# A first phase worked tile by tile: keys and queries directly behind their modulation, in a diffusion layer on one Trainium2 core

## The chip, the cores and the metric

The kernel runs on one core of one Trainium2 chip. The metric is the device time in microseconds of one execution. TensorE (PE) multiplies matrices and loads its weights beside that (PEld); VectorE (DVE), ScalarE (ACT) and GpSimd (POOL) work on tiles; the queue of SyncE (SP) issues nearly all transfers (DMA) from the chip's memory, in program order.

## The reference, cut to what matters

One layer with two token mixers over 256 latent tokens `x` and 256 context tokens `ctx`, D = 2048. Both are normalised and modulated by a shift and a scale that come from a conditioning vector through a large matrix, and then multiplied by the columns of `w_in`. The part that the change touches:

```python
mod = (jax.nn.silu(c) @ w_mod[l] + b_mod[l])[:, None, :]
sa, ca, ga, sm, cm, gm = jnp.split(mod, 6, axis=-1)
mod_c = jax.nn.silu(c_ctx) @ w_mod[l] + b_mod[l]
h_c = modulate(x_ctx, norm_attn_w[l], sa_c, ca_c)     # rmsnorm(x, w) * (1 + scale) + shift
k_c = rmsnorm(split_qk(p_c_kv[..., :QK_WIDTH]), k_norm_w[l])
h = modulate(x, norm_attn_w[l], sa, ca)
p = h @ w_in[l]
q = axial_rope(rmsnorm(split_qk(p[..., Q_OFF:K_OFF]), q_norm_w[l]), row, col)
k = axial_rope(rmsnorm(split_qk(p[..., K_OFF:V_OFF]), k_norm_w[l]), row, col)
```

Values, attention, a pooling mixer, gates, an output product and a squared-ReLU MLP follow; the change does not alter what they compute.

## The kernel before

Every product is computed in three matmuls: each operand is split into a high part (a cast on ScalarE) and a low part (a subtraction on VectorE), and `mm3` adds high x high, high x low and low x high.

Phase one walks over 16 *tiles* f of 128 rows of D. For each tile `mod_tile` multiplies four chunks of `w_m` (512 KB each, 32 short matmuls, "mod") into shift and scale for both kinds of tokens; ScalarE copies them out (`rows`), `mod_columns` turns them into columns (`modT` on TensorE, `col` on ScalarE and VectorE), and `hidden(f, 0)` writes the modulated, transposed tile of x (`hL`, high part on ScalarE, low part on VectorE), `hidden(f, 1)` that of the context (`hC`). Products with the first 512 columns of keys and queries accumulate in six banks over the 16 tiles: `kx` (keys of x), `kc` (keys of the context) and `q` (queries of x). One tile k of one of them, two token halves of 128 with three matmuls each, is six matmuls of 512 columns; the prediction calls this a unit. A chunk of `w_k` or `w_q` holds the weights of two tiles, the pair j = k // 2.

The order of work is set in these places:
- `plan` writes the order of all transfers; `load_next` issues the next one, `wchunk` asks for a chunk and has up to `FIRST_AHEAD` = 3 further ones issued in program order ahead. SP issues in that order, and each transfer waits until its buffer is free.
- Buffers: even tiles' w_m and all chunks of w_k and w_q share one ring of five raw buffers. Odd tiles' w_m have buffers of their own (`mod_raw`: one of two chunks, two of one). `first` holds two split chunks of w_k; w_q, one chunk of w_k and later weights go through three `whi`/`wlo`.
- `side` runs through the products in the order of a list, and `PACE` says how many half units each tile issues, half of them ahead of `modT` and half behind it. The pair j is loaded behind the odd tile 2j + 1 (j = 2 behind tile 6), so its products come two tiles or more behind the modulation.
- `square_sums` squares tokens on ScalarE, adds pairs on VectorE and sums over partitions by matmuls with `mean`; for the context this stands behind `mod` of tile 4.
- A scheduler lays out each engine's instructions from this program order, so the rows of other stages can move as well; TensorE's own order is held in phase one (`ordered_pe`).

Behind phase one, `qk_evac` normalises keys and queries on ScalarE, VectorE and GpSimd (`qraw`, `qsq`, `qss`) and TensorE turns them (`qkT`) in the midst of the v products, a number of chunks later that `later` counts. `macc` are parts of other modulation vectors, computed on VectorE beside all of this.

Of the kernel before, what the change touches and what calls it, by code (L numbers as in the profile page):

```python
# [13 lines left out]
AF = mybir.ActivationFunctionType  # L14
# [5 lines left out]
KT = D // P  # L20
T = 256
# [27 lines left out]
def layer(ctx: ExitStack, tc, a, out):  # L49
# [3 lines left out]
    pe, gp = nc.tensor, nc.gpsimd  # L53
# [20 lines left out]
    def work(name, shape=None, dt=F32):  # L74
        return pool.tile(shape or [P, 512], dt, tag="w2", name=name, bufs=9)
# [42 lines left out]
    def chain(*gens):  # L118
        for g in gens:
            yield from g  # L120
# [5 lines left out]
    def plan(name, *idx, rate=0.0):  # L126
        stream.append(((name,) + idx, rate))
# [3 lines left out]
    for f in range(KT):  # L131
        for i in range(4):
            plan("w_m", f, i)
            if f in (2, 3) and i % 2 == 1:
                plan("cT", 2 * f - 4 + i // 2)
            if (f, i) == (9, 0):
                plan("prq")
        j = 2 if f == 6 else -1 if f == 5 or f % 2 == 0 else f // 2
        if j >= 0:
            plan("w_k", 0, j)  # L140
            plan("w_q", 0, j)
    for n, g, rate in (("w_v", 0, 1.5), ("w_q", 1, 1.0), ("w_k", 1, 1.5), ("w_v", 1, 1.5)):
        for ch in range(8):
            plan(n, g, ch, rate=rate)
# [50 lines left out]
    def load_next():  # L195
        key, rate = stream[len(loaded)]
        src = a[key[0]]
        for i in key[1:]:
            src = src[i]
        if key[0] == "prq":  # L200
            nc.sync.dma_start(prq, src)
            loaded.append((key, None, None))
            return
        if key[0] in ("cT", "x"):
            dst = cT[:, 4 * key[1]:4 * key[1] + 4, :] if key[0] == "cT" else x1_tile()[:, key[1], key[2] * 512:key[2] * 512 + 512]
            nc.sync.dma_start(dst, src)
            loaded.append((key, None, None))
            return
        n = src.shape[-1]
        if key[0] == "w_m":  # L210
            raw = mod_raw(*key[1:])
            sp.dma_start(raw, src)
            loaded.append((key, raw, raw))
            return
        raw = raw_chunk(src, n)
        if key[:2] == ("w_k", 0):
            if not first:
                first.append(s16("first", [P, 4, 1024], F32R))
            i = 2 * (key[2] % 2)
            hi, lo = first[0][:, i, :], first[0][:, i + 1, :]  # L220
        else:
            hi = pool.tile([P, n], F32R, tag="whi", name="whi", bufs=3)
            lo = pool.tile([P, n], F32R, tag="wlo", name="wlo", bufs=3)
        act.copy(hi, raw)  # L224
        vec.tensor_sub(lo, raw, hi.bitcast(F32))  # L225
# [30 lines left out]
    def rsq(v, n, div, tag=None):  # L256

        mk = (lambda nm: small(nm, n)) if n <= 16 else (lambda nm: work(nm, [P, n]))
        y = mk(tag or "rq_y")
        pin(act.activation(y, v, AF.Ln, scale=div * 2.0 ** -64, bias=epsb))  # L260
        act.activation(y, y, AF.Exp, scale=-0.5, bias=ebias)
        t = mk("rq_t")
        vec.scalar_tensor_tensor(t, y, -0.5 * div, y, ALU.mult, ALU.mult)
        vec.scalar_tensor_tensor(t, v, EPS / div, t, ALU.add, ALU.mult)
        vec.scalar_tensor_tensor(y, t, 1.5, y, ALU.add, ALU.mult)
        return y
# [102 lines left out]
    def mod_columns(f, rows):  # L369

        pt = bank("modT")
        for a in range(2):
            pe.matmul(pt[:, 2 * a:2 * a + 2], rows[:, a * P:a * P + P], quads, start=a == 0, stop=a == 1,
                      skip_group_check=True)
        col = small("col", 4)
        act.copy(col, pt[:, 0:4])
        c3 = col.rearrange("p (a c) -> p a c", a=2)
        vec.tensor_add(c3, c3, bias2[:, :, f:f + 1].broadcast_to([P, 2, 2]))
        vec.tensor_scalar(c3[:, 0, :], c3[:, 0, :], pr("nw")[:, f:f + 1], None, ALU.mult)
        return c3  # L380

    def hidden(f, t, c3):

        src, h = ((xT, hL), (cT, hC))[t]
        u = work("hw", [P, T])
        ht, k8 = h[f // 8], f % 8
        bias = c3[:, 1, t:t + 1]
        vec.scalar_tensor_tensor(u, src[:, f, :], c3[:, 0, t:t + 1], rms[t], ALU.mult, ALU.mult)
        act.activation(ht[:, 0, k8, :], u, AF.Identity, bias=bias)
        vec.scalar_tensor_tensor(ht[:, 1, k8, :], u, bias, ht[:, 0, k8, :].bitcast(F32), ALU.add, ALU.subtract)  # L390

    def tokens(nt):
        return [(hL, 0), (hL, 1), (hC, 0), (hC, 1)][:nt]

    def xmm(banks, toks, k, hi, lo, sl, first, last):
        for ps, (h, t) in zip(banks, toks):
            mm3(ps, tok(h, k, 0, t), tok(h, k, 1, t), hi[:, sl], lo[:, sl], first, last)
# [61 lines left out]
    def square_sums(src, eng, sb, i):  # L459

        sq = [work("sq") for _ in range(2)]
        for h in range(2):
            k = 4 * i + 2 * h
            xs = src[:, k:k + 2, :].rearrange("p a t -> p (a t)")
            act.activation(sq[h], xs, AF.Square)
        eng.tensor_add(sq[0], sq[0], sq[1])
        return lambda: [pin(pe.matmul(sb[:, 0:T], mean, sq[0][:, h * T:h * T + T], start=(i + h == 0), stop=(i + h == 4)))
                        for h in range(2)]

    fb = {}  # L470
    held = {}

    def pair_steps(n, j):

        w = "w_q" if n == "q" else "w_k"
        if w not in fb:
            fb[w] = [bank(f"{w}_{t}") for t in range(4 if n != "q" else 2)]
        hi, lo = held[w, j]
        for kk in range(2):
            k = 2 * j + kk  # L480
            for t in range(2):
                t4 = t + (2 if n == "kc" else 0)
                xmm([fb[w][t4]], [tokens(4)[t4]], k, hi, lo, slice(kk * 512, kk * 512 + 512), k == 0, k == KT - 1)
                yield

    def steps(n):
        for _ in range(n):
            next(side, None)

    order = [("kx", 0), ("q", 0), ("kx", 1), ("q", 1), ("kc", 0), ("kc", 1), ("kx", 2), ("q", 2), ("kc", 2)]  # L490
    for j in range(3, 7):
        order += [("kx", j), ("q", j), ("kc", j)]
    side = chain(*(pair_steps(*o) for o in order))
    PACE = (0, 0, 4, 4, 6, 6, 8, 8) + (6,) * 8

    cols = {}

    context = {4: (0, 1), 5: (2, 3, 4), 6: (5, 6)}
    ordered_pe[0] = True
    sb = bank("ssq")  # L500
    for i in range(4):
        square_sums(xT, vec, sb, i)()
    rms = [rsq(sb[:, 0:T], T, P / D, "rms")]
    for f in range(KT):
        if f % 2 == 0:
            ps = bank("mod")
        rows = mod_tile(f, ps)
        if f == 4:
            sb = bank("ssq")
            for i in range(4):  # L510
                square_sums(cT, vec, sb, i)()
            rms.append(rsq(sb[:, 0:T], T, P / D, "rms"))
        j = 2 if f == 6 else -1 if f == 5 or f % 2 == 0 else f // 2
        if j >= 0:
            for w in ("w_k", "w_q"):
                held[w, j] = wchunk(w, 0, j, ahead=FIRST_AHEAD if j < 7 else 1)
        steps(PACE[f] // 2)
        cols[f] = mod_columns(f, rows)
        steps(PACE[f] - PACE[f] // 2)
        hidden(f, 0, cols[f])  # L520
        for k in context.get(f, (f,) if f > 6 else ()):
            hidden(k, 1, cols[k])
        if f == 10:
            tables()
    lasts = [pair_steps(n, 7) for n in ("kx", "q", "kc")]
    for _ in range(2):
        for g in lasts:
            next(g)
            next(g)
    ordered_pe[0] = False  # L530
    kb, qb = fb["w_k"], fb["w_q"]
    qT = s8("qT", [P, NH, T])
    kT = s16("kT", [P, NH, 2 * T])
    for t in range(4):
        qk_evac(kb[t], t, 0, kT, 2, 2 + t)
    for t in range(2):
        qk_evac(qb[t], t, 0, qT, 0, 6 + t)

# [552 lines left out]
```

## Time and profile before

| | us |
|---|---|
| median of 3 runs | 1506.75 |
| lowest and highest | 1505.76, 1507.11 |
| the profiled execution | 1506.33 |
| its span, first to last instruction | 1504.5 |
| granted TensorE clock, mean | 0.991 |
| TensorE busy | 1457.1 (97%) |
| phase one ends (first v matmul) | 147.97 |

The page gives busy times of one profiled execution; matmuls are pipelined and the end of one is modelled, so prices are taken from start to start. The granted clock is the share of full speed that TensorE's clock was given. A row of the timeline is: start, length, engine, line, operation, out<-in, count, and in brackets the idle time before it with what ended it. L67 is the line of a helper through which all matmuls of phase one go.

### The profile page before, as it was taken

What the parts mean: (1) busy time and instruction counts of PE and PEld (TensorE: products, weight loads), DVE (VectorE), ACT (ScalarE), POOL (GpSimd) and SP (SyncE); (2) the same over time, 40 slices, a digit from 0 to 9 for tenths busy, and PEclk for the clock granted to TensorE, in tenths of its full rate; (3) what the DMA queues carried; (4) which work ended last, traced back from release to release, by engine and by line L of the source; (5) the groups of instructions that cost most, each with busy time, mean ns of one, the idle gap of its engine ahead of it and who ended that gap; (6) DMA issues with size and microseconds to landing.
All of it is one profiled execution on the core that took longest, in us unless ns stands there. A gap on an engine that the chain in (4) does not pass through costs nothing.

```text
span 1504.5 us, 20036 instructions
## 1 busy us (share of the span) xinstructions
PE 1457.1 (97%) x7592; PEld 1205.5 (80%) x7592; DVE 992.0 (66%) x1216; ACT 694.6 (46%) x956; POOL 120.7 (8%) x120
## 2 busy tenths in 40 slices
PE   5899999999899999999989999999999999999998
PEld 3567787678878888888879988888888888888887
DVE  3465968877877776666766765666666555555575
ACT  3334344646654444444534545535445453544532
POOL 0000101100320000000000100100000010000260
PEclk8999999999999999999999999999999999999999
DMA  9798687366578778788756677677776666656564
GB/s 377 296 345 324 195 284 247 98 210 208 169 234 295 255 262 273 249 304 282 213 159 203 226 247 239 210 248 229 246 236 215 192 189 194 188 192 193 186 194 141
DMA packets 97440, 347.85 MB, mean 231 GB/s; under 512 B 11072, under 2 KB 11712, under 8 KB 97344
## 3 DMA queue, kind: packets, MB, share of 16 engines
q1 hardware_dynamic: 96768, 345.50, 69.6%
q8 instruction: 59, 0.97, 0.3%
q0 software_dynamic: 576, 1.08, 0.2%
q14 instruction: 37, 0.30, 0.1%
HBM read 344.44 MB, written 2.10 MB: 230 GB/s over the span
## 4 chain that ended last, share of the span: by engine, by line
PE 87%; DVE 4%; DMA 4%; ACT 2%; issue 1%; POOL 1%; SPq 0%; DVEq 0%; ACTq 0%; POOLq 0%
PE f L940 14%; PE f L419 8%; PE f L418 8%; PE f L421 8%; PE f L943 7%; PE pg L419 3%; PE pg L418 3%; PE pg L421 3%; DMA raw<-in_w_m_dram 2%; PE w_k L67 2%; PE wo L419 2%; PE wo L421 2%; PE wo L418 2%; PE pyy L418 2%; PE pyy L419 2%; PE pyy L421 2%
## 5 line engine op out<-in xcount | busy, mean ns | idle before, releaser
L225 DVE TENSOR_TENSOR wlo<-raw,whi 128x1024 fp32r<-128x1024 f32 x443 | 547.9, 1239 | 360.4 <-ACT whi L224 337.6
L224 ACT CAST whi<-raw 128x1024 fp32r<-128x1024 f32 x443 | 463.9, 1048 | 574.2 <-PE f L419 184.9
L940 PE MATMUL f<-h,whi 128*128 128x512 f32 x896 | 224.2, 392 | 0.0
L418 PE MATMUL f<-whi,act 128*128 128x512 f32 x512 | 199.4, 389 | 0.0
L419 PE MATMUL f<-whi,act 128*128 128x512 f32 x512 | 199.3, 389 | 0.0
L940 PEld LDWEIGHTS f<-h,whi 128*128 128x128 f32 x896 | 161.7, 189 | 29.3
L581 DVE SCALAR_TENSOR_TENSOR macc<-raw,sil,macc 128x1024 f32<-128x1024 f32 x128 | 167.5, 1308 | 2.2 <-DMA macc<-in_b_ga_dram 1.9
L421 PE MATMUL f<-wlo,act 128*128 128x512 f32 x512 | 136.8, 389 | 0.0
L943 PEld LDWEIGHTS f<-h,wlo 128*128 128x128 f32 x896 | 122.3, 190 | 8.7
L943 PE MATMUL f<-h,wlo 128*128 128x256 f32 x896 | 124.9, 282 | 0.0
L421 PEld LDWEIGHTS f<-wlo,act 128*128 128x128 f32 x512 | 96.1, 188 | 19.9
L418 PEld LDWEIGHTS f<-whi,act 128*128 128x128 f32 x512 | 96.2, 188 | 19.9
L419 PEld LDWEIGHTS f<-whi,act 128*128 128x128 f32 x512 | 96.2, 188 | 19.7
L418 PE MATMUL pg<-whi,hL 128*128 128x512 f32 x256 | 100.6, 393 | 0.0
L419 PE MATMUL pg<-whi,hL 128*128 128x512 f32 x256 | 99.7, 390 | 0.0
L951 POOL TENSOR_TENSOR rsq<-relu 128x512 f32<-128x512 f32 x28 | 29.1, 1041 | 537.2 <-ACT relu L950 516.9
L421 PE MATMUL pg<-wlo,hL 128*128 128x512 f32 x256 | 68.6, 390 | 1.9 <-DVE wlo L225 1.9
L421 PEld LDWEIGHTS pg<-wlo,hL 128*128 128x128 f32 x256 | 48.0, 188 | 12.3 <-DVE wlo L225 2.4
L418 PEld LDWEIGHTS pg<-whi,hL 128*128 128x128 f32 x256 | 48.1, 188 | 10.1 <-issue 0.2
L419 PEld LDWEIGHTS pg<-whi,hL 128*128 128x128 f32 x256 | 48.1, 188 | 10.1 <-issue 0.2
L418 PE MATMUL wo<-whi,mix 128*128 128x512 f32 x128 | 49.9, 390 | 0.0
L419 PE MATMUL wo<-whi,mix 128*128 128x512 f32 x128 | 49.8, 389 | 0.0
(251 smaller groups left out, 2111.3 us busy)
## 6 DMA issues: line engine op xcount, KB each, us to landing
raw<-in_w_ff_dram SPq DMA_DIRECT2D x240, 512.0 KB, 4.3
raw<-in_w_m_dram SPq DMA_DIRECT2D x64, 512.0 KB, 8.0
raw<-in_w_ga_dram SPq DMA_DIRECT2D x32, 512.0 KB, 4.6
raw<-in_w_cm_dram SPq DMA_DIRECT2D x32, 512.0 KB, 4.4
raw<-in_w_gb_in_dram SPq DMA_DIRECT2D x32, 512.0 KB, 4.5
raw<-in_w_ga_in_dram SPq DMA_DIRECT2D x32, 512.0 KB, 4.7
raw<-in_w_sm_dram SPq DMA_DIRECT2D x32, 512.0 KB, 4.8
raw<-in_w_o_dram SPq DMA_DIRECT2D x32, 512.0 KB, 4.3
```

The source lines that it names most:

```text
L67: return (lambda *a, **k: pin(emit(*a, **k))) if self.flag[0] else emit
L224: act.copy(hi, raw)
L225: vec.tensor_sub(lo, raw, hi.bitcast(F32))
L418: pe.matmul(banks[t], tok(h, k, 0, tt), wt, start=k == 0, stop=False)
L419: pe.matmul(banks[t], tok(h, k, 1, tt), wt, start=False, stop=False)
L421: pe.matmul(banks[t], tok(h, k, 0, tt), wt, start=False, stop=k == 2 * nk - 1)
L581: pin(vec.scalar_tensor_tensor(acc, raw, sil[:, 0, k:k + 1], acc, ALU.mult, ALU.add))
L940: pe.matmul(ps, hi[:, kk * P:kk * P + P], both(h2, k), start=k == 0, stop=False)
L943: pe.matmul(ps[:, T:2 * T], lo[:, kk * P:kk * P + P], act_slice(h2, k, 0), start=False, stop=k == KT - 1)
L951: gp.tensor_mul(sq, r, r)
```

## The change

The transfers of a pair of w_k and w_q now stand directly behind the w_m of its even tile. Products of tiles 0 to 3 on x follow directly on their own modulation (`modulate`, then `products`). From tile 4 on, products of an earlier tile come behind `mod`, the first of them ahead of `modT`: context of tiles 0 and 1 at tile 4, then tile f - 1 at tile f, the context catching up at tiles 7 and 8. At the end the products of tile 15 are left, six half units instead of twelve. The context's squares are added up on VectorE (`context_squares`, at tiles 2 and 3) and summed by one matmul. The third pair of w_k goes through `whi` instead of `first`, so the buffers of `first` are numbered anew. The keys' turning is counted one chunk later (3 + t for 2 + t).

```diff
     for f in range(KT):
         for i in range(4):
             plan("w_m", f, i)
-            if f in (2, 3) and i % 2 == 1:
-                plan("cT", 2 * f - 4 + i // 2)
-            if (f, i) == (9, 0):
-                plan("prq")
-        j = 2 if f == 6 else -1 if f == 5 or f % 2 == 0 else f // 2
-        if j >= 0:
-            plan("w_k", 0, j)
-            plan("w_q", 0, j)
+        if f % 2 == 0:
+            plan("w_k", 0, f // 2)
+            plan("w_q", 0, f // 2)
+        if f in (2, 3):
+            plan("cT", 2 * f - 4)
+            plan("cT", 2 * f - 3)
+        if f == 9:
+            plan("prq")
...
-        if key[:2] == ("w_k", 0):
+        if key[:2] == ("w_k", 0) and key[2] != 2:
...
-            i = 2 * (key[2] % 2)
+            i = 2 * ((key[2] - (key[2] > 2)) % 2)
...
-    order = [("kx", 0), ("q", 0), ("kx", 1), ("q", 1), ("kc", 0), ("kc", 1), ("kx", 2), ("q", 2), ("kc", 2)]
-    for j in range(3, 7):
-        order += [("kx", j), ("q", j), ("kc", j)]
-    side = chain(*(pair_steps(*o) for o in order))
-    PACE = (0, 0, 4, 4, 6, 6, 8, 8) + (6,) * 8
...
+    def context_squares(i):
+        sq = [work("sq") for _ in range(2)]
+        for h in range(2):
+            act.activation(sq[h], cT[:, 4 * i + 2 * h:4 * i + 2 * h + 2, :].rearrange("p a t -> p (a t)"), AF.Square)
+        vec.tensor_add(sq[0], sq[0], sq[1])
+        if total:
+            vec.tensor_add(total[0], total[0], sq[0])
+        else:
+            total.append(sq[0])
+
+    behind = [[("kx", f), ("q", f)] for f in range(4)]
+    behind += [[("kc", 0), ("kc", 1)], [("kx", 4), ("q", 4), ("kc", 2)], [("kx", 5), ("q", 5), ("kc", 3)],
+               [("kx", 6), ("q", 6), ("kc", 4), ("kc", 5)], [("kx", 7), ("q", 7), ("kc", 6), ("kc", 7)]]
+    behind += [[(n, f - 1) for n in ("kx", "q", "kc")] for f in range(9, KT)]
...
     for f in range(KT):
         if f % 2 == 0:
             ps = bank("mod")
         rows = mod_tile(f, ps)
-        if f == 4:
-            sb = bank("ssq")
-            for i in range(4):
-                square_sums(cT, vec, sb, i)()
-            rms.append(rsq(sb[:, 0:T], T, P / D, "rms"))
-        j = 2 if f == 6 else -1 if f == 5 or f % 2 == 0 else f // 2
-        if j >= 0:
-            for w in ("w_k", "w_q"):
-                held[w, j] = wchunk(w, 0, j, ahead=FIRST_AHEAD if j < 7 else 1)
-        steps(PACE[f] // 2)
-        cols[f] = mod_columns(f, rows)
-        steps(PACE[f] - PACE[f] // 2)
-        hidden(f, 0, cols[f])
-        for k in context.get(f, (f,) if f > 6 else ()):
-            hidden(k, 1, cols[k])
+        if f % 2 == 0:
+            for w in ("w_k", "w_q"):
+                held[w, f // 2] = wchunk(w, 0, f // 2, ahead=FIRST_AHEAD)
+        if f < 4:
+            modulate(f, rows)
+        for i, (n, k) in enumerate(behind[f]):
+            products(n, k)
+            if i == 0 and f > 3:
+                modulate(f, rows)
+        if f in (2, 3):
+            for i in range(2):
+                context_squares(2 * f - 4 + i)
+        if f == 3:
+            sq = total[0]
+            vec.tensor_add(sq[:, 0:T], sq[:, 0:T], sq[:, T:2 * T])
+            sb = bank("ssq")
+            pe.matmul(sb[:, 0:T], mean, sq[:, 0:T], start=True, stop=True)
...
-        qk_evac(kb[t], t, 0, kT, 2, 2 + t)
+        qk_evac(kb[t], t, 0, kT, 2, 3 + t)
```

What it moves, at three places. First TensorE at the start, before, from the sums of squares of x (`ssq`) to the first products:

```order
L67 MATMUL ssq<-sq,mean 128x256 x8
L67 MATMUL mod<-raw,cv 32x256 x16
L67 MATMUL modT<-prm,rows 128x2 x2
L67 MATMUL mod<-raw,cv 32x256 x16
L67 MATMUL modT<-prm,rows 128x2 x2
L67 MATMUL mod<-raw,cv 32x256 x16
L67 MATMUL w_k_249<-first,hL_92 128x512 x3
L67 MATMUL w_k_250<-first,hL_92 128x512 x3
```

TensorE at the start, now:

```order
L67 MATMUL ssq<-sq,mean 128x256 x8
L67 MATMUL mod<-raw,cv 32x256 x16
L67 MATMUL modT<-prm,rows 128x2 x2
L67 MATMUL w_k_186<-first,hL_92 128x512 x3
L67 MATMUL w_k_187<-first,hL_92 128x512 x3
L67 MATMUL w_q_196<-whi,hL_92 128x512
L67 MATMUL w_q_196<-wlo,hL_92 128x512
```

The products of tile 0 stand ahead of `mod` of tile 1, and wait there for their own `modT` and what follows from it.

Second, SP's queue from the first chunk of tile 10 on, before (raw_733 to raw_791 are tile 10's four chunks, raw_793 to raw_871 tile 11's; the words in brackets name the engines or landings that a transfer waits for):

```order
L212 DMA raw_733<-in_w_m_dram 128x1024 [waits DMAHW4_49,PE_49]
L212 DMA raw_753<-in_w_m_dram 128x1024 [waits DMAHW5_49,PE_49]
L212 DMA raw_755<-in_w_m_dram 128x1024 [waits DMAHW6_49,PE_49]
L212 DMA raw_791<-in_w_m_dram 128x1024 [waits DMAHW7_49,DMAHW2_49,DVE_49]
L212 DMA raw_793<-in_w_m_dram 128x1024 [waits DMAHW0_49,PE_49]
L212 DMA raw_793<-in_w_m_dram 128x1024 [waits DMAHW1_49]
L212 DMA raw_796<-in_w_m_dram 128x1024 [waits PE_49]
L212 DMA raw_871<-in_w_m_dram 128x1024 [waits DMAHW3_49,PE_49]
L115 DMA raw_873<-in_w_k_dram 128x1024 [waits DMAHW4_49,PE_49]
L115 DMA raw_877<-in_w_q_dram 128x1024 [waits DMAHW5_49,DVE_49]
```

SP's queue from the first chunk of tile 10 on, now (raw_750 to raw_808 are tile 10's, raw_820 to raw_898 tile 11's):

```order
L212 DMA raw_750<-in_w_m_dram 128x1024 [waits DMAHW4_49,PE_49]
L212 DMA raw_752<-in_w_m_dram 128x1024 [waits DMAHW5_49,PE_49]
L212 DMA raw_806<-in_w_m_dram 128x1024 [waits DMAHW6_49,PE_49]
L212 DMA raw_808<-in_w_m_dram 128x1024 [waits DMAHW7_49,DVE_49]
L115 DMA raw_810<-in_w_k_dram 128x1024 [waits DMAHW0_49,DVE_49]
L115 DMA raw_814<-in_w_q_dram 128x1024 [waits DMAHW4_49,DMAHW1_49,PE_49]
L212 DMA raw_820<-in_w_m_dram 128x1024 [waits DMAHW2_49]
L212 DMA raw_820<-in_w_m_dram 128x1024 [waits DMAHW3_49]
L212 DMA raw_841<-in_w_m_dram 128x1024
L212 DMA raw_898<-in_w_m_dram 128x1024 [waits DMAHW5_49]
```

The pair's two chunks moved ahead of the odd tile's four, and w_q there waits for TensorE, which has to read the buffer of tile 10's first chunk.

Third, TensorE behind phase one, before, around the first turning of keys (v_0 to v_3 are the banks of the v products):

```order
L418 MATMUL v_3_1350<-whi,hC_94 128x512
L419 MATMUL v_3_1350<-whi,hC_94 128x512
L418 MATMUL v_0_1347<-whi,hL_92 128x512
L419 MATMUL v_0_1347<-whi,hL_92 128x512
L453 MATMUL qkT<-prm,qraw 128x128 x4
L418 MATMUL v_1_1348<-whi,hL_92 128x512
```

The same place, now:

```order
L421 MATMUL v_1_1359<-wlo,hL_92 128x512
L421 MATMUL v_2_1360<-wlo,hC_94 128x512
L421 MATMUL v_3_1361<-wlo,hC_94 128x512
L453 MATMUL qkT<-prm,qraw 128x128 x4
L418 MATMUL v_0_1358<-whi,hL_92 128x512
L419 MATMUL v_0_1358<-whi,hL_92 128x512
```

The first `qkT` moved from the tenth matmul of the second v chunk to that chunk's end, 43 matmuls behind the last product of phase one instead of 34; five of the v matmuls of the first chunk stand among the last products.

More of the change, by code (lines that the diff above doesn't have):

```diff
@@ L471, in layer, with products @@
     held = {}
-    def pair_steps(n, j):
+    def products(n, k):
         w = "w_q" if n == "q" else "w_k"
@@ L477, in pair_steps @@
             fb[w] = [bank(f"{w}_{t}") for t in range(4 if n != "q" else 2)]
[L478 to L488, printed above, removed]
-    order = [("kx", 0), ("q", 0), ("kx", 1), ("q", 1), ("kc", 0), ("kc", 1), ("kx", 2), ("q", 2), ("kc", 2)]
-    for j in range(3, 7):
-        order += [("kx", j), ("q", j), ("kc", j)]
-    side = chain(*(pair_steps(*o) for o in order))
-    PACE = (0, 0, 4, 4, 6, 6, 8, 8) + (6,) * 8
+        hi, lo = held[w, k // 2]
+        c = (k % 2) * 512
+        for t in range(2):
+            t4 = t + (2 if n == "kc" else 0)
+            xmm([fb[w][t4]], [tokens(4)[t4]], k, hi, lo, slice(c, c + 512), k == 0, k == KT - 1)
     cols = {}
-    context = {4: (0, 1), 5: (2, 3, 4), 6: (5, 6)}
     ordered_pe[0] = True
@@ L503, in layer, with modulate @@
     rms = [rsq(sb[:, 0:T], T, P / D, "rms")]
+    total = []
+    def context_squares(i):
[11 more added lines that the diff above has]
+    behind += [[(n, f - 1) for n in ("kx", "q", "kc")] for f in range(9, KT)]
+    context = {4: (2, 3), 5: (4,), 6: (5,), 7: (6, 7)}
+    def modulate(f, rows):
+        cols[f] = mod_columns(f, rows)
+        hidden(f, 0, cols[f])
+        for k in context.get(f, (f,) if f > 7 else ()):
+            hidden(k, 1, cols[k])
     for f in range(KT):
@@ L507, in layer @@
         rows = mod_tile(f, ps)
-        if f == 4:
+        if f % 2 == 0:
[13 more added lines that the diff above has]
+            vec.tensor_add(sq[:, 0:T], sq[:, 0:T], sq[:, T:2 * T])
             sb = bank("ssq")
-            for i in range(4):
-                square_sums(cT, vec, sb, i)()
+            pe.matmul(sb[:, 0:T], mean, sq[:, 0:T], start=True, stop=True)
             rms.append(rsq(sb[:, 0:T], T, P / D, "rms"))
-        j = 2 if f == 6 else -1 if f == 5 or f % 2 == 0 else f // 2
-        if j >= 0:
-            for w in ("w_k", "w_q"):
-                held[w, j] = wchunk(w, 0, j, ahead=FIRST_AHEAD if j < 7 else 1)
-        steps(PACE[f] // 2)
-        cols[f] = mod_columns(f, rows)
-        steps(PACE[f] - PACE[f] // 2)
-        hidden(f, 0, cols[f])
-        for k in context.get(f, (f,) if f > 6 else ()):
-            hidden(k, 1, cols[k])
+            for k in range(2):
+                hidden(k, 1, cols[k])
         if f == 10:
             tables()
[L525 to L529, printed above, removed]
+    for n in ("kx", "q", "kc"):
+        products(n, KT - 1)
     ordered_pe[0] = False
```

## The prediction

> **What bounds the kernel now.** I read the page first, for the split by engine:
>
> ```profile
> PE 1457.1 (97%) x7592; PEld 1205.5 (80%) x7592; DVE 992.0 (66%) x1216; ACT 694.6 (46%) x956; POOL 120.7 (8%) x120
> ```
>
> TensorE is busy for 97% of the span, so what is worth having is the 3% where it is not. The windows view of the first 170 us shows where much of that lies (window, length, then busy us of PE, PEld, DVE, ACT, POOL, granted clock, DMA share, GB/s):
>
> ```profile
> 16.00:19.40 3.40, 2.42 (x28) 0.99 (x28) 1.44 (x5) 0.71 (x3) 0.00 (x0) 1.00 1.02 408
> 19.40:22.80 3.40, 1.28 (x16) 0.68 (x12) 0.61 (x3) 1.32 (x3) 0.00 (x0) 0.99 1.04 413
> 22.80:33.00 10.20, 5.68 (x35) 1.97 (x36) 3.04 (x4) 1.98 (x4) 0.00 (x0) 0.50 1.01 393
> 33.00:50.00 17.00, 10.94 (x94) 5.97 (x92) 5.08 (x10) 4.39 (x9) 0.00 (x0) 1.00 0.85 328
> 50.40:56.60 6.20, 5.11 (x12) 4.11 (x13) 2.77 (x4) 3.45 (x7) 0.00 (x0) 0.50 1.03 415
> 56.60:96.00 39.40, 39.40 (x301) 28.70 (x300) 22.42 (x60) 14.55 (x31) 0.00 (x0) 1.00 0.82 303
> 96.00:148.00 52.00, 50.74 (x371) 36.22 (x371) 27.39 (x59) 22.04 (x44) 0.00 (x0) 1.00 0.92 345
> 148.00:170.00 22.00, 19.81 (x93) 15.88 (x92) 22.00 (x47) 11.25 (x25) 3.18 (x2) 1.00 0.45 143
> ```
>
> Up to 57 us PE idles for half of the time, on DMA at its full 410 GB/s, and twice at half clock. From 56.6 to 96 it never idles, to 148 it idles 1.3 us. So phase one has two halves: transfers bound the first, TensorE the second, with little to spare on either side. From 148 to 170 VectorE is full and PE idles 2.2 us. Third view, the timeline, for prices:
>
> ```profile
> 13.58 2.02 PE L67 MATMUL mod<-raw,cv 128*32 128x256 f32 x32
> 14.28 0.33 SPq L115 DMA_DIRECT2D raw<-in_w_q_dram  x1
> 15.67 0.37 ACT L366 COPY rows<-mod 128x256 f32<-128x256 f32 x1 [0.97 <-PE mod L67]
> 16.73 0.16 ACT L376 COPY col<-modT 128x4 f32<-128x4 f32 x1 [0.70 <-PE modT L67]
> 17.46 0.48 DVE L388 SCALAR_TENSOR_TENSOR hw<-xT,col,rms 128x256 f32<-128x256 f32 x1
> 18.58 0.48 DVE L390 SCALAR_TENSOR_TENSOR hL<-hw,col,hL 128x256 fp32r<-128x256 f32 x1 [0.64 <-ACT hL L389]
> 18.79 0.64 PE L67 MATMUL mod<-raw,cv 128*32 128x256 f32 x8 [0.63 <-DMA raw<-in_w_m_dram]
> 20.08 0.64 PE L67 MATMUL mod<-raw,cv 128*32 128x256 f32 x8 [0.65 <-DMA raw<-in_w_m_dram]
> 21.91 1.05 ACT L224 CAST first<-raw 128x1024 fp32r<-128x1024 f32 x1
> 22.99 1.22 DVE L225 TENSOR_TENSOR first<-raw,first 128x1024 fp32r<-128x1024 f32 x1
> 50.66 0.69 DVE L466 TENSOR_TENSOR sq<-sq 128x512 f32<-128x512 f32 x1 [4.68 <-ACT sq L465]
> 51.49 6.35 PE L67 MATMUL ssq<-sq,mean 128*128 128x256 f32 x16 [2.35 <-DVE sq L466]
> 84.92 1.94 PE L67 MATMUL mod<-raw,cv 128*32 128x256 f32 x32
> 86.78 2.33 PE L67 MATMUL w_k<-first,hL 128*128 128x512 f32 x9
> 91.54 1.93 PE L67 MATMUL mod<-raw,cv 128*32 128x256 f32 x32
> 142.53 1.52 PE L67 MATMUL w_k<-first,hC 128*128 128x512 f32 x6
> 143.89 1.52 PE L67 MATMUL w_k<-first,hL 128*128 128x512 f32 x6
> 147.97 0.39 PE L418 MATMUL v<-whi,hL 128*128 128x512 f32 x1
> ```
>
> The prices, with the name of each in the sums:
> - A *unit* (six matmuls, one k, one of kx, q, kc): 143.89 - 142.53 = 1.36 us, 0.227 a matmul.
> - A tile's `mod`: 86.78 - 84.92 = 1.86. The whole tile with three units: 91.54 - 84.92 = 6.62, so 4.76 behind `mod`, and 6.12 with a fourth unit.
> - A *chunk* (512 KB) at full rate: 20.08 - 18.79 = 1.29, taken as 1.28.
> - The *chain* from a tile's rows to its modulated low part: 15.67 to 18.58 + 0.48, 3.4 us.
> - The queue's *release*: the first quarter of `mod` begins at 13.58, and the q transfer that needs its buffer starts at 14.28: 0.7.
> - A cast with its low part: 1.05 + 1.22.
> - Phase one ends where v begins, 147.97.
>
> The chain of waits prices a transfer that begins with an empty queue:
>
> ```profile
> 44.87 3.59 DMA raw<-in_w_m_dram
> ...
> 96.14 3.78 DMA raw<-in_w_m_dram
> ...
> 109.89 4.27 DMA raw<-in_w_m_dram
> ...
> 124.14 3.78 DMA raw<-in_w_m_dram
> ```
>
> I take 3.7, between the lowest and the two that agree, and 1.28 for every chunk behind the first.
>
> **What the change costs and gives.** *Products earlier.* When tile 8 begins, before has done 18 units (36 of its half-unit steps), after 20. That is work taken out of the second half, worth 2.7 us, if after gets there no later.
>
> *Context's squares.* 8 matmuls on `mean` become 1. The 8 cost 6.35 us of PE at half clock and 2.35 us of waiting ahead of them. One stays, 0.8 at that rate, 0.4 at full clock; four 512-wide adds of 0.69 and one half as wide come on VectorE, which is under half busy there. They are not free: they stand in front of the one matmul and of `mod` of tile 4.
>
> *The pair's q transfer now stands ahead of the next tile.* This is the price. The raw ring has five buffers, an even tile takes six (four w_m, k, q), so q always waits for the first quarter of its own tile's `mod`. Before, q stood behind the odd tile's w_m, and those went out in time. Now the four w_m chunks of the odd tile stand behind it on SP. The odd tile's last chunk lands at start of the even tile + 0.7 + 3.7 + 4 x 1.28 = + 9.5, its `mod` ends + 0.64 later. TensorE by itself would be there at 1.86 + 4.76 + 1.86 = 8.5. So a pair takes 9.5 + 0.64 + 4.76 = 14.9 us, where TensorE alone needs 13.24 and before took 14.2 and 13.8 (the last three landings in the chain above, at 99.92, 114.16 and 127.92).
>
> *The sum, tile by tile, S(f) being the start of tile f's `mod`.* Tile 0's w_m still lands at 15; its chain is delayed by k's low part, which VectorE now does first, to 16.9 + 1.05 + 1.22 + 0.48 = 19.7. Then 12 matmuls at 0.227 (2.7 us) or, at half clock, 0.454 (5.4 us). The clock is the unknown: it closed at 22.8 after a 3.4 us window with 1.28 us of work, and stayed open after one with 2.42. After will have about 1 us between 16 and 19.4 (`modT` and the first matmuls). I take the middle, 4.05 us, for the twelve behind the waits of tiles 0, 1 and 3, and keep both ends. So tile 0 ends at 23.75, `mod` of tile 1 at 25.6, chain 3.4, products: S(2) = 33.1. There q is released: 33.8, landing 37.5; two context chunks and four w_m behind it: 45.2, `mod` of tile 3 ends 45.9. (Tile 2's products begin at 37.5 + 1.05 + 1.22 + 0.48 = 40.2 and at half clock end 45.6: hidden.) Chain and products: 53.4. VectorE's adds end before that (last context chunk at 47.8, five adds, 3.1 us, the chain's operations between). Matmul: S(4) = 54.0. Tile 5's last chunk 54.0 + 9.5 = 63.5, `mod` ends 64.1; kc of 0 and 1 lie in that wait. S(6) = 68.9, tile 7's `mod` ends 79.0, four units: S(8) = 85.1, against 84.92. Tile 8 has four units, so TensorE (94.9) and the landing (95.2) meet: S(10) = 100.0. Then 14.9 twice: S(14) = 129.8; tile 15's `mod` ends 140.0; 4.76, and three units, 4.1: 148.8. Against 147.97: **0.9 us later**. The two units of lead are eaten by the pairs.
>
> *Behind phase one.* The kernel before waits there for keys to be turned:
>
> ```profile
> 157.15 0.66 PE L453 MATMUL qkT<-prm,qraw 128*128 128x128 f32 x4 [1.31 <-POOL qraw L446]
> 162.13 0.65 PE L453 MATMUL qkT<-prm,qraw 128*128 128x128 f32 x4 [0.89 <-POOL qraw L446]
> ```
>
> The view of waits sums them over the next 110 us, and the chain shows what stood in their way on VectorE:
>
> ```profile
> PE qkT L453 <- POOL qraw L446: 2.8, 3, 1.3
> ```
>
> ```profile
> 149.95 1.20 DVE macc L581
> ...
> 152.57 1.20 DVE macc L581
> ```
>
> After, 43 v matmuls, not 34, stand between the last product and the first transposes, and these two `macc` come behind the first key on VectorE. The first key was turned at 157.15, 9.2 us behind phase one; less 2.4 that is 6.8, and 43 matmuls take 9.8. So the waits go: 1.31 + 0.89 = 2.2 by the two rows, 2.8 by the sum of waits. I take 2.5, ends 0 and 2.8. The five v matmuls put ahead of the last products are moved, not added. `first` and `whi` buffers come free in time in the new numbering, tile by tile, so I cost that edit at nothing: the last user of each is at least a tile ahead of the next cast. The rest of the kernel keeps its work; a few late sums stand elsewhere, which I cost at 0, +-1.5.
>
> Sum: +0.9 - 2.5 = -1.6. The profiled execution took 1506.33, the median is 1506.75, 0.4 above it; from the median, **1505.1**. The measurement can tell about 0.2%, 3 us.
>
> **A rule against the trace.** The Trainium skill ("TensorE: Matmul & The Clock Gate", What's actually happening) has the clock halved after an idle window of about 3.4 us, and restored after as long a busy one. Taken strictly, tiles 0, 1 and 3 have no wholly idle window, the clock stays open and the forecast would be 1501. Here the trace differs: the window from 19.4 to 22.8 held 1.28 us of work and the clock still fell. The same skill ("DMA: Bandwidth & Descriptors", Latency and other measured facts) gives about 2 us of fixed cost per transfer; with 1.28 that is an estimate of 3.3 for mine of 3.7, and seven places at 0.4 would take 2.8 us off. The rows say 3.59 at least.
>
> **Rivals.**
> - *The clock stays open in tiles 0, 1 and 3.* For: 2.42 us of work kept it open. Against: after's windows hold less. Three times 1.35 less: S(4) = 50, all behind it 4 us earlier: 1501. At half clock throughout: 1509.
> - *The pair loop does not form*, because landings overlap the wait better than my sum: TensorE is packed from tile 6 on. The waits of tiles 7, 9 and of 11, 13, 15 go: 1.6 + 0.3 + 3 x 1.66 = 6.9: 1498.2. Against: before's own pairs wait at just such landings, and the ring is the same.
> - *Slower: q's transfer and the four behind it need longer from an empty queue.* The price is seven-fold (tiles 2 to 14). At the start of the kernel four chunks took from 1.18 to 9.80:
>
> ```profile
> 1.18 1.84 SPq L275 DMA_DIRECT2D xT<-in_xT_dram  x4
> 2.60 7.20 DMA xT<-in_xT_dram
> ```
>
> That is 8.6 us where I count 3.7 + 3 x 1.28 = 7.5. So up to 1.1 x 7 = 7.7 us: 1512.8. Against: the first transfers carry prm ahead of them, and 3.59 to 3.78 is what three of four rows say. It decides from 0.66 us a place on (4.6 in all): a landing of 4.4, just above the worst row, makes the kernel slower by 0.2%.
>
> **Chances.** My sum with its neighbours, within 0.2%: 0.45. Open clock 0.27 and packed pairs 0.11, both faster: 0.38. Slow landings: 0.17. The range leaves out the packed pairs and half of the slow landings: 1499 to 1511.
>
> **What will show it.** Right: SP issues each w_q right behind the first quarter of an even `mod`; PE waits for w_m in the odd tiles 5, 7, 11, 13, 15, one to two us each; v begins near 148; no wait at `qkT`; granted clock 0.5 in parts of 20 to 50 us. Wrong: even tiles less than 14 us apart; tile 8 begins far from 85; a DMA queue that is never empty between 29 and 34 us.

## The result, and the profile after

| | median, us | lowest to highest | ratio to before, 95% interval |
|---|---|---|---|
| before | 1505.91 | 1504.14 to 1507.11 | |
| changed | 1511.07 | 1508.64 to 1514.71 | 1.0039 [1.0030, 1.0047] |

The change makes the kernel slower by 0.39%; forecast were 1505.1 us, a range of 1499 to 1511 and no difference. The profiled execution took 1510.03 us, with a span of 1507.7 (1504.5 before) and a mean clock of 0.987. The page of the changed kernel, split by engine:

```profile
PE 1458.5 (97%) x7578; PEld 1206.2 (80%) x7578; DVE 993.4 (66%) x1220; ACT 694.3 (46%) x956; POOL 122.4 (8%) x120
```

TensorE is busy 1.4 us longer than before (1457.1); most of the time is lost in waits. The windows view of the changed kernel, four of the stretches shown of before (window, length, busy us of PE, PEld, DVE, ACT, POOL, granted clock, DMA share, GB/s):

```profile
19.40:22.80 3.40, 3.40 (x18) 2.39 (x20) 1.04 (x1) 0.00 (x0) 0.00 (x0) 0.71 1.00 402
22.80:33.00 10.20, 7.80 (x68) 5.13 (x63) 1.36 (x4) 1.04 (x3) 0.00 (x0) 0.83 0.57 229
...
56.60:96.00 39.40, 35.48 (x248) 24.00 (x252) 20.19 (x42) 14.32 (x30) 0.00 (x0) 0.96 0.87 328
96.00:148.00 52.00, 46.83 (x365) 30.26 (x358) 23.61 (x63) 16.45 (x33) 0.00 (x0) 0.97 0.90 349
```

In the first two PE works more than before (3.40 for 1.28, 7.80 for 5.68) and at a clock between half and full. From 56.6 to 96 PE was full before and now idles 3.9 us; to 148 it idles 5.2 instead of 1.3. From 148 to 170 it is the other way: full now (22.00 us), 2.2 idle before. The timeline of TensorE in the changed kernel: starts of tiles 4, 6, 8, 10, 12 and 14, the last quarter of `mod` in the odd tiles 5, 7, 11, 13 and 15, and what is behind phase one:

```profile
53.07 1.93 PE L67 MATMUL mod<-raw,cv 128*32 128x256 f32 x32
63.62 0.64 PE L67 MATMUL mod<-raw,cv 128*32 128x256 f32 x8 [0.64 <-DMA raw<-in_w_m_dram]
68.94 1.93 PE L67 MATMUL mod<-raw,cv 128*32 128x256 f32 x32
79.64 1.08 PE L67 MATMUL mod<-raw,cv 128*32 128x256 f32 x8 [0.64 <-DMA raw<-in_w_m_dram]
80.65 2.65 PE L67 MATMUL w_k<-first,hL 128*128 128x512 f32 x6
87.80 1.93 PE L67 MATMUL mod<-raw,cv 128*32 128x256 f32 x32
102.73 1.93 PE L67 MATMUL mod<-raw,cv 128*32 128x256 f32 x32
112.94 0.64 PE L67 MATMUL mod<-raw,cv 128*32 128x256 f32 x8 [0.64 <-DMA raw<-in_w_m_dram]
118.32 1.93 PE L67 MATMUL mod<-raw,cv 128*32 128x256 f32 x32
128.26 0.64 PE L67 MATMUL mod<-raw,cv 128*32 128x256 f32 x8 [0.66 <-DMA raw<-in_w_m_dram]
133.58 1.93 PE L67 MATMUL mod<-raw,cv 128*32 128x256 f32 x32
144.15 1.02 PE L67 MATMUL mod<-raw,cv 128*32 128x256 f32 x8 [0.64 <-DMA raw<-in_w_m_dram]
145.09 2.83 PE L67 MATMUL w_k<-first,hL 128*128 128x512 f32 x6
156.15 0.39 PE L418 MATMUL v<-whi,hC 128*128 128x512 f32 x1
165.90 0.60 PE L453 MATMUL qkT<-prm,qraw 128*128 128x128 f32 x4
```

Tiles 10, 12 and 14 begin 15.6 and 15.3 us apart, where 14.9 was forecast and TensorE alone needs 13.24. Five v matmuls stand ahead of the last products, so these end at 156.15 - 5 x 0.227 = 155.0: 7.0 later than before. The first `qkT` has no wait in brackets; nor have the other three of the keys, and one of 0.65 us is left at the first `qkT` of the queries (184.92). SP's issues of the same pairs, and, from the view of the tensor, the time from issue to landing of w_q (six transfers between 50 and 136 us):

```profile
53.77 0.33 SPq L115 DMA_DIRECT2D raw<-in_w_q_dram  x1
69.64 0.33 SPq L115 DMA_DIRECT2D raw<-in_w_q_dram  x1
103.43 0.33 SPq L115 DMA_DIRECT2D raw<-in_w_q_dram  x1
119.02 0.33 SPq L115 DMA_DIRECT2D raw<-in_w_q_dram  x1
134.28 0.33 SPq L115 DMA_DIRECT2D raw<-in_w_q_dram  x1
```

```profile
L115 SPq DMA_DIRECT2D raw<-in_w_q_dram x6: 327/328/328, 53.8 to 134.3; - x6
DMA to landing us min/median/max: 3.6/3.7/4.1
```

From the issue of q to the last quarter of the odd tile's `mod`: 9.85, 10.0, 9.5, 9.2 and 9.9 us. The prediction had 3.7 + 4 x 1.28 = 8.8. The 3.7 holds (only tile 6's q took 4.1); most of the rest is in the four chunks. The same view for the first, the second and the last of tile 11's four (an issue, then its time to landing):

```profile
L212 SPq DMA_DIRECT2D raw<-in_w_m_dram x1: 423/423/423, 103.8 to 103.8; - x1
DMA to landing us min/median/max: 4.6/4.6/4.6
...
L212 SPq DMA_DIRECT2D raw<-in_w_m_dram x1: 422/422/422, 104.3 to 104.3; - x1
DMA to landing us min/median/max: 6.1/6.1/6.1
...
L212 SPq DMA_DIRECT2D raw<-in_w_m_dram x1: 737/737/737, 105.2 to 105.2; - x1
DMA to landing us min/median/max: 7.7/7.7/7.7
```

q lands at 107.1, the first at 108.4, the second at 110.4, the last at 112.9: steps of 1.3, 2.0 and, for two chunks, 2.5. One step is 0.7 us too long. Windows of the changed kernel over the first two steps:

```profile
107.13:108.41 1.28, 1.28 (x8) 1.05 (x7) 1.14 (x5) 1.21 (x2) 0.00 (x0) 1.00 0.97 362
108.41:110.38 1.97, 1.58 (x14) 0.67 (x12) 1.97 (x5) 0.46 (x2) 0.00 (x0) 1.00 1.03 420
```

The transfer engines did not pause in the long step: 1.97 us at 420 GB/s are 0.83 MB, while one chunk of 0.52 MB landed. The surplus can only belong to chunks that landed later; which, the windows do not tell.

### The profile page after: what moved, and what is told of

Its sections match the earlier page's. It is cut to its first block, busy times and chain, and to the rows that moved or that the text cites. A ratio compares the mean times of both kernels' runs of the same rounds, so it can differ in the third digit from the quotient of the medians.

```text
span 1507.7 us, 19990 instructions
## 1 busy us (share of the span) xinstructions
PE 1458.5 (97%) x7578; PEld 1206.2 (80%) x7578; DVE 993.4 (66%) x1220; ACT 694.3 (46%) x956; POOL 122.4 (8%) x120
## 3 DMA queue, kind: packets, MB, share of 16 engines
q0 software_dynamic: 576, 1.08, 0.3%
## 4 chain that ended last, share of the span: by engine, by line
PE 88%; DVE 4%; DMA 4%; ACT 2%; POOL 1%; issue 1%; SPq 1%; DVEq 0%; ACTq 0%; POOLq 0%
PE f L955 14%; PE f L419 8%; PE f L418 8%; PE f L421 8%; PE f L958 7%; PE pg L421 4%; PE pg L418 4%; PE pg L419 4%; DMA raw<-in_w_m_dram 3%; PE w_k L67 2%; PE pyy L418 2%; PE wo L419 2%; PE wo L418 2%; PE wo L421 2%; PE pyy L421 2%; PE pyy L419 2%
## 5 line engine op out<-in xcount | busy, mean ns | idle before, releaser
L225 DVE TENSOR_TENSOR wlo<-raw,whi 128x1024 fp32r<-128x1024 f32 (+1 forms) x444 | 548.6, 1238 | 362.4 <-ACT whi L224 346.2
L224 ACT CAST whi<-raw 128x1024 fp32r<-128x1024 f32 (+1 forms) x444 | 464.8, 1048 | 570.9 <-PE f L419 178.2
```

## The experiments

All ratios are to the kernel before, measured on the same chip in the same session; versions of different sessions compare by their ratios.

| version | median, us | ratio, 95% interval |
|---|---|---|
| changed, q in a buffer of its own | 1496.58 | 0.9943 [0.9930, 0.9955] |
| changed, waits of odd tiles filled | 1510.54 | 1.0034 [1.0022, 1.0047] |
| before, squares on VectorE | 1502.81 | 0.9982 [0.9973, 0.9992] |
| before, keys turned later | 1502.67 | 0.9980 [0.9971, 0.9988] |
| changed, q behind four w_m | 1497.71 | 0.9947 [0.9933, 0.9962] |
| changed, q behind two w_m | 1499.76 | 0.9960 [0.9945, 0.9975] |
| changed, q behind one w_m | 1504.82 | 0.9998 [0.9988, 1.0007] |
| changed, q on ScalarE's queue | 1511.24 | 1.0040 [1.0025, 1.0054] |
| before, squares and keys | 1500.84 | 0.9966 [0.9953, 0.9978] |
| before, squares, keys, q's buffer | 1496.83 | 0.9942 [0.9929, 0.9956] |
| the same, sum behind tile 4's `mod` | 1491.50 | 0.9912 [0.9897, 0.9926] |

**The changed kernel, with w_q of phase one outside the ring.**

```diff
-        raw = raw_chunk(src, n)
+        if key[:2] == ("w_q", 0):
+            raw = pool.tile([P, 1024], F32, tag="macc", name="raw", bufs=1)
+            sp.dma_start(raw, src)
+        else:
+            raw = raw_chunk(src, n)
```

> The changed kernel with one edit: the raw chunks of w_q of phase one go into the macc buffer, which nothing uses until phase one ends, instead of the ring of five. Queue, program order and products stay. Theory (the pair loop: w_q waits on SP for its own tile's mod, and holds the odd tile's w_m behind it): that wait is gone, TensorE is packed from tile 4 on, tile 8 begins near 80 instead of 87.8, pairs take 13.2 to 13.6 us, phase one ends near 138 instead of 155, the kernel takes 1493 to 1497. Rival (the chains of tiles 0 to 3 and the clock are what costs): tile 8 still begins near 86, 1507 or more.

1496.58, 14.5 us under the changed kernel. Windows of its second half of phase one, and where phase one ends:

```profile
56.60:96.00 39.40, 39.40 (x299) 28.09 (x299) 23.68 (x62) 15.54 (x33) 0.00 (x0) 1.00 0.98 378
96.00:135.60 39.60, 39.60 (x325) 28.31 (x325) 21.44 (x48) 16.40 (x32) 1.62 (x2) 1.00 0.94 352
```

```profile
140.84 0.39 PE L422 MATMUL v<-whi,hC 128*128 128x512 f32 x1
```

In these windows TensorE is never idle and its granted clock is 1.00; products end at 140.84 - 5 x 0.227 = 139.7, 15.3 us earlier than in the changed kernel. One buffer takes away the whole loss and more.

**The changed kernel with its odd tiles' waits filled.** From tile 5 on, the first quarter of an odd tile's `mod` is multiplied three times more ahead of itself; the real matmuls overwrite the result.

```diff
+        for _ in range(3 if f % 2 and f > 4 else 0):
+            for j in range(4):
+                pe.matmul(ps[32 * j:32 * j + 32, c:c + T], cv[:, j, :], raws[0][:, j * T:j * T + T],
+                          start=True, stop=True)
```

> The changed kernel with 12 further short matmuls (mod of the first quarter, three times over, overwritten by the real one) ahead of mod in the odd tiles from 5 on: TensorE works where it waited for w_m. Theory (waits of the loop close the clock in tiles 7 and 15, which run their products at half speed): the landings stay where they are, 1.4 us come back behind each of the two tiles, 1507 to 1509, and the runs lie closer together than the changed kernel's 1508.6 to 1514.7. Rival (the clock costs nothing, the landings all): 1510 to 1512 with the same spread.

1510.54, within the rival's numbers. Windows around tiles 7 and 15 of this version, and one behind its tile 4:

```profile
73.00:83.00 10.00, 9.25 (x87) 6.14 (x85) 4.51 (x8) 3.17 (x6) 0.00 (x0) 1.00 1.01 390
139.00:149.00 10.00, 9.37 (x86) 6.27 (x86) 5.45 (x10) 4.56 (x8) 0.00 (x0) 1.00 1.02 404
```

```profile
58.85:62.26 3.41, 3.41 (x11) 2.46 (x9) 3.33 (x6) 1.62 (x3) 0.00 (x0) 0.50 0.98 363
```

At tiles 7 and 15 the clock stayed open, as meant, and in this trace the time came back there: from the end of tile 7's `mod` to tile 8 it takes 6.1 us (7.5 in the changed kernel), from the end of tile 15's to the last product 8.7 (10.2). The version spends as much elsewhere. Tile 4 begins 0.5 later. In the pair of tiles 4 and 5 it loses 0.8, with the clock at half as the last window shows. In the pair of 8 and 9 it loses 1.0, because tile 9 had no wait to fill and the added matmuls are plain work there. In the pair of 12 and 13 it loses 1.3, because the last quarter of tile 13's `mod` came 10.5 us behind its q (119.54 to 130.03), not 9.2. Products end at 154.9. So this run doesn't price the clock: what it won at two tiles it paid for at others.

**The kernel before with one part each.** First the context's squares summed on VectorE as in the change:

```diff
-        if f == 4:
-            sb = bank("ssq")
-            for i in range(4):
-                square_sums(cT, vec, sb, i)()
+        if f in (2, 3):
+            for i in range(2):
+                context_squares(2 * f - 4 + i)
+        if f == 3:
+            sq = total[0]
+            vec.tensor_add(sq[:, 0:T], sq[:, 0:T], sq[:, T:2 * T])
...
```

> The kernel before with the context's squares alone changed (added up on VectorE at tiles 2 and 3, one matmul with mean behind tile 3). Theory: 2.35 us of waiting and 6 us of half-clock matmuls at 51 to 57 us go, less 0.8; the transfers of tile 5 are there by then, so most of it is kept: 3 to 7.5 us faster, 1498.5 to 1503. Rival: the next w_m take the place of the wait, no change, 1505 to 1507.

1502.81, as expected. The theory left out one thing: in this trace the one matmul on `mean` now waits 6.82 us for VectorE. Then the keys:

```diff
-        qk_evac(kb[t], t, 0, kT, 2, 2 + t)
+        qk_evac(kb[t], t, 0, kT, 2, 3 + t)
```

> The kernel before with the keys' turning alone counted one chunk later (3 + t). Theory: the two waits of TensorE at qkT go, 1.5 to 2.8 us faster. Rival: VectorE is full there and the wait shows up at wlo, no change within 0.5 us.

1502.67. Timeline of this version, where phase one ends and where the second group's queries begin, and the wait at `qkT` over the next 110 us:

```profile
146.27 0.39 PE L418 MATMUL v<-whi,hL 128*128 128x512 f32 x1
...
192.67 0.39 PE L418 MATMUL q<-whi,hL 128*128 128x512 f32 x1
```

```profile
PE qkT L453 <- POOL qraw L446: 0.2, 1, 0.2
```

46.4 us lie between the two rows; the kernel before has 197.03 - 147.97 = 49.1. So the part is worth 2.7 in the trace, close to the 2.5 of the prediction; the other 0.9 of the median's 3.6 lies ahead of it or in the scatter.

**The same two together.** Both edits above.

> The kernel before with two parts of the change and no others: context's squares summed on VectorE, and the keys turned one chunk later. If the two are independent, their gains measured alone (3.4 and 3.6 us) add: 1497.5 to 1501. Then all the rest of the change (single tiles, early products, q ahead of the odd tile) costs some 12 us. Rival (both remove the same slack): 1502 to 1503, and the rest costs some 8 us.

1500.84: the parts add up (0.9982 x 0.9980 = 0.9962, measured 0.9966, within its interval). All the rest of the change costs 1.0039 / 0.9966 = 1.0073, 11 us.

**These two and w_q's own buffer**, again without single tiles and early products.

> The same two parts on the kernel before, and w_q of phase one in a buffer of its own. Against the changed kernel with that buffer (1496.6) this lacks only the early products by single tiles. If these are worth the two units of lead that were counted (2.7 us): 1498.5 to 1500.5. If they are worth nothing: 1496 to 1497.5. If the kernel before had no wait that the buffer takes away, this equals the kernel with the two parts alone.

1496.83, the same as the changed kernel with that buffer (1496.58). Early products by single tiles show no gain here, though the intervals would hide one of 2 to 3 us. In the order of before the buffer is worth 4.0 us (1500.84 to 1496.83), so of its 14.5 in the changed kernel some 10.5 belong to the place of q that the change chose. Timeline of this version, TensorE at the end of the context's sum, and the first v matmul:

```profile
47.63 1.19 PE L67 MATMUL ssq<-sq,mean 128*128 128x256 f32 x2 [6.81 <-DVE sq L538]
...
140.05 0.39 PE L422 MATMUL v<-whi,hL 128*128 128x512 f32 x1
```

It starts tile 4 at 48.8, 4.1 us ahead of the changed kernel with the buffer (52.9), with fewer products done, and ends phase one 0.4 us behind it (140.05 and 139.7).

**q behind the odd tile's w_m.** From tile 4 on w_q is planned and taken behind all four w_m of the odd tile, with context ahead of queries in each tile:

```diff
-        if f % 2 == 0:
-            plan("w_k", 0, f // 2)
-            plan("w_q", 0, f // 2)
+        if f % 2 == 0:
+            plan("w_k", 0, f // 2)
+        if f in (0, 2) or f > 4 and f % 2 == 1:
+            plan("w_q", 0, f // 2)
...
-    behind += [[(n, f - 1) for n in ("kx", "q", "kc")] for f in range(9, KT)]
+    behind += [[(n, f - 1) for n in ("kx", "kc", "q")] for f in range(9, KT)]
...
```

> The changed kernel with one move: from tile 4 on the pair's w_q transfer stands behind the four w_m transfers of the odd tile on SP instead of ahead of them, and within each tile the context products come ahead of the queries. The ring of five stays, and q still waits for the first quarter of the even tile's mod. Loop theory (q holds the four w_m behind it in an in-order queue, and they land at start + 0.7 + 4.6 + 4 x 1.28): the w_m are out early, TensorE is packed from tile 5 on at 6.62 us a tile, tile 8 begins at 81.5, phase one ends at 140, time 1495 to 1498. Rival (the five-buffer ring or the transfer rate holds the pairs, whatever the order): pairs stay near 15 us, 1507 or more.

1497.71. The ring of five is kept, and its window of the second half shows TensorE all but full:

```profile
96.00:136.00 40.00, 39.87 (x325) 28.07 (x325) 21.39 (x54) 15.86 (x32) 0.00 (x0) 1.00 1.00 391
```

So it is the place in the queue, not the ring by itself. Next, one w_m ahead of q and three behind:

```diff
         for i in range(4):
+            if f > 4 and f % 2 == 1 and i == 1:
+                plan("w_q", 0, f // 2)
             plan("w_m", f, i)
...
```

> The changed kernel with w_q, from tile 4 on, behind the first of the odd tile's four w_m: three w_m stay behind it instead of four (context products ahead of the queries, as in the version with q behind all four: 1497.7). The pair's law, last landing at start + 0.7 + first landing + 3 x 1.28, against 8.5 for TensorE. With a first landing of 4.6 us, as the changed kernel's trace shows: 9.1, a pair takes 14.5 instead of 13.24, six pairs lose 1.3 each: 1504 to 1506. With the 3.7 of the prediction: 8.2, TensorE is packed: 1497 to 1499.

1504.82, in the band for the longer landings, but by luck, because two things in that text were wrong. The 4.6 was reckoned back from the last landings; the transfers' own times, above, say 3.7 for q and one long step behind it. And 8.2 against 8.5 left out the last quarter's 0.64: with the prediction's prices a pair would take 0.7 + 3.7 + 3 x 1.28 + 0.64 + 4.76 = 13.6, 0.4 more than TensorE, 1500 and not 1498. The measured time is still some 4 to 5 us above that. Timeline of this version, tiles 10 to 14:

```profile
102.07 1.93 PE L67 MATMUL mod<-raw,cv 128*32 128x256 f32 x32
...
111.71 0.64 PE L67 MATMUL mod<-raw,cv 128*32 128x256 f32 x8 [1.52 <-DMA raw<-in_w_m_dram]
...
117.03 1.93 PE L67 MATMUL mod<-raw,cv 128*32 128x256 f32 x32
...
125.45 0.64 PE L67 MATMUL mod<-raw,cv 128*32 128x256 f32 x8 [0.29 <-DMA raw<-in_w_m_dram]
...
130.81 1.93 PE L67 MATMUL mod<-raw,cv 128*32 128x256 f32 x32
```

One pair takes 15.0, the next 13.8: the long step falls among the three chunks of the first and behind those of the second.

Last, two ahead and two behind (the same with i == 2):

> The same with w_q behind two of the odd tile's w_m, two behind it. With 4.6 us: last landing at 7.9, before TensorE's 8.5, packed: 1497 to 1499. If the pairs still lose a us each, the landing is not 4.6 plus 1.28 for each chunk, and something else than the number of transfers behind q sets it.

1499.76, a little above the band: it is nearly packed, with 1.9 us of waits for w_m left from tile 4 on in its trace. With four, three, two and none behind q the ratios are 1.0039, 0.9998, 0.9960 and 0.9947 (medians 1511.1, 1504.8, 1499.8 and 1497.7). The loss goes with the number of transfers that stand behind q. The last three versions also multiply context ahead of queries, which was not run alone; q's own buffer without that order is as fast (0.9943).

**q on another queue.** From pair 2 on ScalarE issues w_q; ring, release and order of the work stay.

```diff
+        if key[:2] == ("w_q", 0) and key[2] > 1:
+            raw = pool.tile([P, n], F32, tag="raw", name="raw", bufs=5)
+            nc.scalar.dma_start(raw, src)
+        else:
+            raw = raw_chunk(src, n)
```

> The changed kernel with the w_q transfers of pairs 2 to 7 issued from ScalarE's queue instead of SP's; buffers, order of the work and the release of q's buffer stay as they are. Loop theory, in its narrowest form (it is the in-order queue and nothing else): the odd tile's w_m no longer wait for q, TensorE is packed, 1495 to 1498; ScalarE stands still until q's buffer is free, a few tenths of a us a pair, hidden. Rival (q's late buffer itself, or the transfer's landing, sets the pair's time): products of q wait instead, 1505 or more.

1511.24, against the loop theory in the form written there. The longest waits in phase one from 56 us on, of PE and for a transfer on ScalarE, in the trace, which is of an execution of 1506.93 us:

```profile
PE w_k L67 <- ACT hL L393: 6.9, 4, 3.1
```

```profile
ACT whi L228 <- DMA raw<-in_w_q_dram: 14.1, 6, 3.1
```

The waits of `mod` for w_m are gone altogether, so the queue did hold them. But ScalarE now stands 14.1 us ahead of the cast of w_q, whose landing takes up to 7.6 us beside SP's transfers, and the modulated tile (`hL`) behind it comes late. The waiting changed its engine: products end at 149.8 here, 10.1 behind the version with q's own buffer. What the others waited for, up to 1518.52 us, is in no trace.

**The best version.** From the one with squares, keys and q's buffer, the block `if f == 3` with the sum's one matmul moves behind `mod_tile`, as `if f == 4`.

> The kernel before with the squares on VectorE, the keys turned later and w_q in its own buffer (1496.8), and the one matmul on the mean put behind tile 4's mod, which until then stood behind its wait of 6.8 us for VectorE. If mod of tile 4 (1.9 to 3 us) goes into that wait: 1493.5 to 1495.5. If its w_m or the context's first product comes late instead: 1496 to 1497.5.

1491.50, better than expected: 0.88% under the kernel before. In its timeline the 6.81 us wait for VectorE is down to 0.88, since tile 4's `mod`, with 2.5 us of waits for its own w_m, lies in it now:

```profile
48.05 1.19 PE L67 MATMUL ssq<-sq,mean 128*128 128x256 f32 x2 [0.88 <-DVE sq L527]
```

That explains only a part. The trace is of an execution of 1495.49 us, the longest of the six, and phase one ends there at 138.51, 1.5 us earlier than without the move; the ratios differ by 0.0030, 4.5 us. Four of the other executions had a mean clock of 0.991 to 0.993, against 0.989 at most without the move. So the rest may be clock, but no trace shows where.

## Why the prediction was wrong, step by step

**Phase one up to tile 4: right, but for the start.** Tile 2 was forecast at 33.1 and began at 31.97, tile 4 at 54.0 and began at 53.07. The 0.9 us is the start of the trace: tile 0's `mod` began at 12.68, in the kernel before at 13.58. The twelve products of tiles 0, 1 and 3 took 4.5 to 4.7 us, between the middle clock that was taken (4.05) and half clock (5.4). Tile 6 at 68.94 for 68.9 is luck: the early start and a late landing in tile 5 cancel.

**The pairs: the right mechanism, the wrong size.** That a pair takes some 15 us because the four w_m stand behind q is what the trace shows and what moving q out of the way proves. The term that failed is 3.7 + 4 x 1.28 = 8.8 from the issue of q to the odd tile's last chunk, and in it "1.28 for every chunk behind the first". q itself lands after 3.6 to 4.1 us, and most steps are 1.28, but each time the queue is filled anew one step among the first is up to 0.9 us longer. Tiles 5, 7, 11, 13 and 15 got their last chunk 1.05, 1.2, 0.7, 0.4 and 1.1 us later than summed: 4.45 us. A row that hinted at this was on the table: four chunks at the start of the kernel took 8.6 and not 7.5 (in the changed kernel's trace the same four took 7.7). It was put into the rival "slow landings" with 17%, for the argument that three of four landings in the chain took 3.6 to 3.8; those rows price the first landing, not the ones behind it. The point from which that rival decides, 0.66 us a place, was passed on average (4.45 / 5 = 0.9), but at five places, not seven: 4.45 us is just short of 7 x 0.66 = 4.6, and the next term did the rest.

**A term that was missing: the clock in the waits.** Behind tile 7's `mod` the trace has 87.80 - 80.28 = 7.5 us where 6.12 was summed, behind tile 15's 155.0 - 144.79 = 10.2 where 8.9 was: the waits that the forecast itself put there closed the clock (1.08 and 1.02 for the last quarter, not 0.64; 2.65 and 2.83 for six matmuls, not 1.65). That is 2.7 us of this trace. How much of it the median holds stays open: the version with filled waits wins it back at these two tiles, but loses as much at others, and its median is only 0.5 us lower, with intervals that overlap.

With 0.9 for the early start of tile 4, -0.9 + 4.45 + 2.7 = 6.25: the phase ended at 155.0, forecast 148.8, a difference of 6.2.

**Products earlier: wrong.** The lead of two units was counted at 2.7 us "if after gets there no later". Without the queue's loss no gain is seen (1496.58 and 1496.83): tile 8 begins with two units, 2.7 us, more done, but 2.4 us later (81.40 against 79.02).

**The keys: right in kind, smaller in size.** The waits of the keys are gone, and one of 0.65 us is left at the queries; 2.5 was forecast. The part alone shows 2.7. In the changed kernel the second group's queries begin at 202.27, 47.2 behind the end of phase one instead of 49.1: 1.8. Over all that is behind phase one the changed kernel gains 3.7: its last product stands at 1502.07, 1347.1 behind the end of phase one, before at 1498.72, 1350.7 behind. 7.0 - 3.7 = 3.3 is the difference of the spans to 0.1. The 1.9 beyond the queries is spread over later stages and has no experiment.

**The sum** was therefore +7.0 - 3.7 instead of +0.9 - 2.5. That is of single traces; the medians lie 5.2 us apart, and the changed kernel's trace is of an execution of 1510.03 us. What those of 1512.7 to 1514.7 us lost is in no trace.

**The rules weighed.** The Trainium skill ("TensorE: Matmul & The Clock Gate", What's actually happening) closes the clock after an idle window of some 3.4 us. Here it closed without one. Windows of the changed kernel, the 3.4 us ahead of the fall at tile 7, the same length behind it, one at tile 11, and the one ahead of the fall at tile 15:

```profile
76.01:79.42 3.41, 1.66 (x24) 0.32 (x16) 1.30 (x4) 0.51 (x1) 0.00 (x0) 1.00 1.01 407
79.42:82.83 3.41, 3.19 (x13) 2.00 (x14) 0.00 (x0) 0.37 (x1) 0.00 (x0) 0.50 1.03 413
110.14:113.55 3.41, 1.88 (x25) 0.51 (x25) 1.36 (x7) 0.71 (x2) 0.00 (x0) 1.00 1.04 417
140.85:144.27 3.42, 1.40 (x20) 0.44 (x24) 0.87 (x2) 0.51 (x1) 0.00 (x0) 1.00 1.02 413
```

With 1.66 and 1.40 us of work the clock fell; with 1.88 at tile 11, in much the same waits, it stayed open. The version with filled waits kept it open at tiles 7 and 15 and lost it at tile 5, at 58.85, behind 3.4 us with 1.66 of work. The skill's "DMA: Bandwidth & Descriptors" (Queues, rings and completion order) says that each of the 16 engines takes its share of the transfers in order, but that transfers do not complete strictly one after the other. That agrees with the long step, in which 0.83 MB moved while 0.52 MB landed. But the chunks still landed in their order of issue, and the single engines are not seen in these runs, so it is not shown to be the cause, which stays open.

## What to carry to other kernels

Before a transfer is moved up in an in-order queue, look at what its buffer waits for: everything behind it inherits that wait, and then comes from an empty queue. A spare buffer, or a place behind the transfers that are free to go, cost nothing here and were worth 14 us. Price a refilled queue by a row in which several transfers land behind the first one, and give each wait that a forecast predicts its own clock.

## What the hardware showed that was not expected

- A queue that starts empty does not deliver its chunks at an even 1.28 us. In the five pairs of the changed kernel that waited, one of the four steps behind q was 1.6 to 2.2 us, at full transfer rate.
- The clock halves without an idle window. In the changed kernel it fell behind 3.4 us with 1.66 or 1.40 us of work and stayed at full behind 1.88. Repeated matmuls kept it open at the two tiles where it had fallen.
- The changed kernel's times follow the clock: of the 14 executions those with a mean clock of 0.987 took 1508.6 to 1511.3 us, those with 0.985 and 0.986 took 1512.7 to 1514.7.
